# Up projection: product 2 of two neighbouring pairs as seven half-size block products

## The chip, the core and the metric

The kernel runs on one core of a Trainium2 chip. The core has a matrix engine (TensorE, PE in the profile, with its weight loads shown apart as PEld), a vector engine (VectorE, DVE), a scalar engine (ScalarE, ACT), a general one (GpSimd, POOL) and SyncE (SP), which here only issues transfers. Matmul results land in PSUM, eight banks of 512 float32 per partition; all else lives in SBUF or in device memory. The metric is the time of one execution on the device in microseconds, as the median of several runs.

## The reference

Two layers of an encoder over 1040 frames (16 learned ones and 1024 of input) with 1024 channels. In each layer an attention part (gated linear attention and softmax attention) is followed by a gated feed-forward part, and only the latter matters here:

```python
def conv_ffn(x, w_up, conv_w, conv_b, w_down):
    h = x @ w_up                        # 1040 x 1024 times 1024 x 5632
    L = h.shape[1]
    hp = jnp.pad(h, ((0, 0), (CONV_W - 1, 0), (0, 0)))
    hc = conv_b
    for j in range(CONV_W):             # causal, width 3, per channel
        hc = hc + hp[:, j:j + L] * conv_w[j]
    u, g = jnp.split(hc, 2, axis=-1)
    return (jax.nn.silu(g) * u) @ w_down
```

All is float32. The hidden width of 2816 is 22 tiles of 128 channels, once for u and once for g.

## The kernel before

Channels lie on partitions, frames along the free dimension. A float32 product is made of three matmuls in a reduced float32 format (`mm3`, lines 218 to 224): each operand is split into a high part (a cast on ScalarE) and a low part (a subtraction on VectorE), and hi*hi, lo*hi and hi*lo are summed in PSUM.

The up projection of a layer (`ffn_up`, from line 1076) goes over 22 pairs j of a u tile and a g tile. For each pair the product of 256 output channels by 1024 input channels with the 1040 frames is seen as a 2 x 2 block product: output u or g, input channels lower or upper half, frames first or second half (`t0`, `t1`, 520 frames each; 516 in the last layer). It is taken as seven block products p = 1 to 7 in place of eight, by the Strassen-Winograd scheme. One block product has 512 input channels, 128 outputs and 520 frames: four weight blocks of 128 x 128, two pieces of 260 frames, three matmuls each, 24 matmuls in all.

The weight operands of the seven products are A11, A12 (u, lower and upper channels), A22, A21 (g), and the combinations S1, S2 and so on, made on VectorE in `block_operand` (line 1037, the combinations at line 1055) and split in `up_split` (line 1067: the cast at 1072 gives hi, the subtraction at 1073 gives lo). The raw tiles come by SyncE's transfers (line 1045). The moving operands X[1] to X[7] are the same for all pairs, and are made once per layer at its start (`put`, line 1094).

Product 2 is A12 with X[2], the upper channels of the first half of the frames. It goes to u's first half only: C11 = P1 + P2.

The order of PE's work is the list `seq` (lines 1101 to 1107), written out by hand. From the sixth pair on a pair's part of it is

```python
(j, 2), (j, 6), (j, 5), (j, 7), (j + 1, 1), (j, 4), (j, 3)
```

The operand of a product is requested four places ahead in this list (`AHEAD`, `ensure`). Its hi and lo tiles rotate through six pairs of buffers, three in each of two pools by turns, so a split can start when the product six places earlier is done. Raw weight tiles have four buffers (`raw`) for A11 and A12, and seven (`raw2`) for the rest. PE works strictly in the order written; the instructions of the other engines are put in order, ahead of the run, by a planner that simulates them with a cost model, and each engine then works through its own list.

PSUM is four double banks, p0 to p3. Products 1, 6, 7, 4 of a pair accumulate in one double bank ("a", p0 or p1 by turns) and are read after each step; 5 and 3 share p2 ("x"), and 2 has p3 ("y"). The results are taken out by ScalarE copies (line 1264) and VectorE adds (line 1263) into two SBUF tiles, `hu` and `hg`. After product 3 the pair is complete, and `conv` (line 1249) does the width-3 convolution: a ScalarE activation (line 1252) and two VectorE steps (line 1256) for each of u and g, then a SiLU on ScalarE (line 1283), a product on VectorE (line 1287), and a store to device memory (line 1288).

During the last pair the operands that are no longer needed give their SBUF slots back, and `during_last` (`tail` in `ffn_down`) uses them to load and split the first inputs of the down projection (lines 337 and 1381), which follows at once. There are 33 slots of 1040 float32 per partition, and 6 more in this part of the layer; the seven moving operands take 28 of them.

Of the kernel before, what the change touches and what calls it, by code (L numbers as in the profile page):

```python
# [25 lines left out]
NFF = 22  # L26
# [13 lines left out]
M_GK, M_GQ, M_GV, M_GR, M_REM, M_FQ, M_FK, M_FV, M_WO, M_UP = 0, 2, 4, 8, 12, 13, 17, 21, 25, 33  # L40
# [8 lines left out]
GROUPS, LAST = (("n", 0, 3), ("s", 3, 8), ("r", 11, 4), ("r", 15, 4)), (19, 3)  # L49
HALVES, HALVES_LAST, HALVES_OUT = (0, 520, 520), (8, 524, 516), (16, 528, 512)  # L50
AHEAD = 4
NSPLIT = 4
N_DMA_SUM = 5
WARM = 12


# [79 lines left out]
class Kern:  # L136
# [893 lines left out]
    def up_operand(self, lyr, j, p, fw, raws, odd):  # L1030
        if (j, p) in ((2, 1), (2, 2), (3, 2), (4, 2)):
            src = fw.tile([128, 4, 128], F32, tag="raw2", name="raw2")
            self.nc.sync.dma_start(src[:], self.wm[lyr, M_UP + 2 * j][:, 4 * p - 4:4 * p, :])
            return self.up_split(src, fw, odd)
        return self.block_operand(self.wm[lyr, M_UP + 2 * j], self.wm[lyr, M_UP + 2 * j + 1], 4, j, p, fw, raws, odd, j < N_DMA_SUM)

    def block_operand(self, u, g, nk, j, p, fw, raws, odd, by_dma=False):

        nc = self.nc
        if j not in raws:  # L1040
            q = raws[j] = {}
            for name, src, k0, own in (("A11", u, 0, True), ("A21", g, 0, False), ("A22", g, nk, False), ("A12", u, nk, True)):
                q[name] = self.wp.tile([128, 4, 128], F32, tag="raw", name="raw", bufs=4) if own else \
                    fw.tile([128, 4, 128], F32, tag="raw2", name="raw2")
                nc.sync.dma_start(q[name][:, :nk, :], src[:, k0:k0 + nk, :])
            if by_dma:
                q["S1"] = fw.tile([128, 4, 128], F32, tag="raw2", name="raw2")
                nc.sync.dma_start(q["S1"][:], g[:, 0:4, :])
                nc.gpsimd.dma_start(q["S1"][:], g[:, 4:8, :], accum_op=ALU.add)
        q = raws[j]  # L1050
# [25 lines left out]
    def ffn_up(self, lyr, mix, hT, pp, fw, halves, o0, during_last):  # L1076
        nc, s = self.nc, self.slots
        W = halves[2]
        n = W // 2
        sl = [slice(c, c + W) for c in halves[:2]]  # L1080
        gain = lambda k: self.v(lyr, V_FN, k)
        bank2 = lambda name, i: pp.tile([128, 2, 512], F32, tag=f"p{i}", name=name, bufs=1)
# [3 lines left out]
        half_slot = lambda name: s.get(F32, name, (128, 2, 520))  # L1086


        X = {}
# [154 lines left out]
        before = {1: second_half, 2: make_t2, 7: make_t3, 8: make_n4, 11: make_t1, 14: make_b22}  # L1244


        st = {}

        def conv(hb, idx):
            t = s.get(F32, "cv")  # L1250
# [7 lines left out]
            s.put(hb)  # L1258
            return t

        def evacuate(j, p):
            q = st[j]
            add = lambda out, ps: nc.vector.tensor_tensor(out=two(out), in0=used(ps), in1=two(out), op=ALU.add)  # L1263
            copy = lambda out, bank="a": nc.scalar.copy(two(out), used(q[bank]))
            if p in (1, 2):
                bank = "a" if p == 1 else "y"
                if "u" in q:
                    add(q["u"][:, t0], q[bank])
                else:
                    q["u"] = s.get(F32, "hu")  # L1270
                    copy(q["u"][:, t0], bank)
            elif p == 6:
                copy(q["u"][:, t1])
            elif p == 7:
                q["g"] = s.get(F32, "hg")
                copy(q["g"][:, t1])
            elif p == 4:
                copy(q["g"][:, t0])
            elif p == 3:
                add(q["u"][:, t1], q["x"])  # L1280
                u, g = conv(q["u"], j), conv(q["g"], j + NFF)
                uo, go = u[:, o0:T], g[:, o0:T]
                nc.scalar.activation(go, go, AF.Silu)
                if j == NFF - 1:
                    self.preload = self.tc.keep_in_program_order(
                        nc.scalar.preload_act_table_set("natural_log_exp_and_others"))
                nc.vector.tensor_tensor(out=uo, in0=uo, in1=go, op=ALU.mult)  # L1287
                nc.gpsimd.dma_start(self.actd[j][:, o0:T], uo)  # L1288
                s.put(u, g)
                del st[j]  # L1290
# [128 lines left out]
    def down_blocks(self, lyr, g0, ng, X, pp, fw, halves, after):  # L1419
# [345 lines left out]
```

## Time and profile before

| | |
|---|---|
| median of 3 runs | 2515.2 us (2514.78 to 2515.3) |
| the profiled execution | 2518.04 us, span 2516.3 us |
| matmuls | 18442, of which 7392 in the up projection |
| up projection, layer 0 | 568 to 1013 us |
| up projection, layer 1 | 1812 to 2260 us |
| mean granted TensorE clock | 0.996 |

The profile's page gives, for each engine, the busy time and its share of the span. A row of its groups or of the timeline names the line of the program, the engine, the operation, the tiles (written tile first, then an arrow and what is read) and the shape; after a bar stand the busy time, the mean duration and the idle time of the engine just before, with what ended it. A row of the windows gives, for each stretch of time, the busy time and the number of instructions of each engine, the granted clock, the share of the transfer engines and GB/s. Matmul durations overlap, because the engine is pipelined; what counts is the distance from start to start.

### The profile page before, as it was taken

To read this page: it belongs to the slowest core of one execution; us is meant where nothing else is said; L and a number is where in the kernel's file an instruction comes from. 1 tells how busy PE (TensorE), PEld (TensorE's weight loads), DVE (VectorE), ACT (ScalarE), POOL (GpSimd) and SP (SyncE) were. 2 spreads that over 40 slices of the span, in tenths; PEclk is the share of its full clock that TensorE was granted. 3 is DMA by queue.
4 is the path that set the end of the run, shared out by engine and by line. 5 is a ranking of instruction groups with operands and counts; after the bars stand their busy time and mean duration, and the time that the engine had idled before them with its cause. 6 is when DMAs were issued, how large, how long until landed. Compare 5 with 4: busy or idle time off the path is not lost.

```text
span 2516.3 us, 47049 instructions
## 1 busy us (share of the span) xinstructions
PE 2477.9 (98%) x18442; PEld 2383.8 (95%) x18442; DVE 1767.2 (70%) x3523; ACT 1272.9 (51%) x2733; POOL 385.3 (15%) x567
## 2 busy tenths in 40 slices
PE   9999999999999999999999999999999999999998
PEld 8999999999999999999999899999999999997786
DVE  8656777769877777853666666777798777787535
ACT  7346666636544445631443566665464444455312
POOL 2023433210000000100211234331100000001002
PEclk9999999999999999999999999999999999999999
DMA  3232134343322224763312222143433222258722
GB/s 133 67 88 74 44 92 133 118 130 97 119 81 81 77 77 146 193 170 106 107 57 69 74 80 78 58 153 109 142 105 101 76 79 78 80 166 186 194 56 74
DMA packets 118542, 260.94 MB, mean 104 GB/s; under 512 B 14880, under 2 KB 32544, under 8 KB 118320
## 3 DMA queue, kind: packets, MB, share of 16 engines
q1 hardware_dynamic: 93984, 182.79, 23.5%
q0 software_dynamic: 22464, 72.84, 10.4%
q8 instruction: 144, 2.36, 0.4%
q10 hardware_dynamic: 1872, 2.31, 0.3%
q14 instruction: 78, 0.64, 0.1%
HBM read 177.29 MB, written 67.81 MB: 97 GB/s over the span
## 4 chain that ended last, share of the span: by engine, by line
PE 81%; DVE 10%; ACT 4%; DMA 2%; issue 2%; SPq 0%; POOL 0%; DVEq 0%; ACTq 0%; POOLq 0%
PE up L222 11%; PE up L224 11%; PE up L223 11%; PE mm L222 7%; PE mm L224 7%; PE mm L223 7%; PE down L222 5%; PE down L223 5%; PE down L224 5%; PE av L720 3%; PE tr L694 2%; DVE S L661 1%; PE S L658 1%; ACT P L673 1%; PE S L659 1%
## 5 line engine op out<-in xcount | busy, mean ns | idle before, releaser
L222 PE MATMUL up<-x,hi 128*128 128x260 f32 (+1 forms) x2464 | 696.6, 283 | 0.0
L224 PE MATMUL up<-x,hi 128*128 128x260 f32 (+1 forms) x2464 | 695.9, 282 | 0.7 <-DVE x L1097 0.7
L223 PE MATMUL up<-x,lo 128*128 128x260 f32 (+1 forms) x2464 | 696.3, 283 | 0.0
L224 PEld LDWEIGHTS up<-x,hi 128*128 128x128 f32 x2464 | 465.3, 189 | 1.1 <-DVE x L1097 1.1
L222 PEld LDWEIGHTS up<-x,hi 128*128 128x128 f32 x2464 | 464.5, 189 | 0.4 <-DVE hu L1263 0.2
L223 PEld LDWEIGHTS up<-x,lo 128*128 128x128 f32 x2464 | 464.5, 189 | 0.1
L1073 DVE TENSOR_TENSOR lo<-raw,hi 128x512 fp32r<-128x512 f32 x364 | 247.7, 685 | 173.0 <-ACT hi L1072 172.7
L222 PE MATMUL mm<-xh,hi 128*128 128x348 f32 (+4 forms) x1056 | 362.7, 343 | 0.0
L224 PE MATMUL mm<-xl,hi 128*128 128x348 f32 (+4 forms) x1056 | 339.8, 322 | 0.0
L223 PE MATMUL mm<-xh,lo 128*128 128x348 f32 (+4 forms) x1056 | 339.4, 321 | 0.0
L1072 ACT CAST hi<-raw 128x512 fp32r<-128x512 f32 x364 | 223.6, 620 | 128.1 <-PE up L224 84.5
L222 PEld LDWEIGHTS mm<-xh,hi 128*128 128x128 f32 x1056 | 199.5, 189 | 5.2 <-issue 4.6
L223 PEld LDWEIGHTS mm<-xh,lo 128*128 128x128 f32 x1056 | 199.5, 189 | 0.7 <-issue 0.7
L224 PEld LDWEIGHTS mm<-xl,hi 128*128 128x128 f32 x1056 | 198.3, 188 | 0.4 <-issue 0.3
L189 ACT CAST hi<-raw 128x512 fp32r<-128x512 f32 (+2 forms) x168 | 97.4, 581 | 176.0 <-PE down L224 97.0
L223 PE MATMUL down<-ah,lo 128*128 128x260 f32 (+1 forms) x528 | 168.6, 319 | 0.4 <-DVE lo L191 0.3
L224 PE MATMUL down<-al,hi 128*128 128x260 f32 (+1 forms) x528 | 168.5, 319 | 0.0
L222 PE MATMUL down<-ah,hi 128*128 128x260 f32 (+1 forms) x528 | 168.2, 319 | 0.0
L673 ACT ACTIVATE P<-S,m 116x460 f32<-116x460 f32 (+2 forms) x224 | 124.8, 561 | 71.2 <-DVE m L661 67.6
L337 DVE TENSOR_TENSOR PT<-tr,PT 116x464 fp32r<-116x464 f32 (+3 forms) x240 | 122.8, 514 | 46.9 <-ACT PT L336 45.3
L1055 DVE TENSOR_TENSOR raw<-raw,raw 128x512 f32<-128x512 f32 x198 | 129.4, 684 | 17.2 <-DMA raw<-in_wd_dram 16.5
L1288 POOL DMA_DIRECT2D actd<-cv x44 | 23.6, 535 | 756.9 <-DVE cv L1287 735.9
(289 smaller groups left out, 5623.8 us busy)
## 6 DMA issues: line engine op xcount, KB each, us to landing
raw<-in_wm_dram SPq DMA_DIRECT2D x330, 256.0 KB, 2.7
raw<-in_wd_dram SPq DMA_DIRECT2D x64, 256.0 KB, 3.6
actd<-cv POOLq DMA_DIRECT2D x22, 520.0 KB, 3.0
actd<-cv POOLq DMA_DIRECT2D x22, 512.0 KB, 2.9
cb<-cd SPq DMA_DIRECT2D x16, 520.0 KB, 4.1
st<-actd SPq DMA_DIRECT2D x14, 520.0 KB, 4.9
st<-actd SPq DMA_DIRECT2D x14, 512.0 KB, 4.6
kA<-kA SPq DMA_DIRECT2D x24, 260.0 KB, 3.9
```

The source lines that it names most:

```text
L189: nc.scalar.copy(hi[:, :n, :], raw[:, :n, :])
L222: nc.tensor.matmul(ps, wh, xh[:, c0:c0 + n], start=first, stop=False, skip_group_check=more)
L223: nc.tensor.matmul(ps, wl, xh[:, c0:c0 + n], start=False, stop=False, skip_group_check=more)
L224: nc.tensor.matmul(ps, wh, xl[:, c0:c0 + n], start=False, stop=last, skip_group_check=more)
L337: nc.vector.tensor_tensor(out=lo, in0=src, in1=hi.bitcast(F32), op=ALU.subtract)
L658: nc.tensor.matmul(S[:rows, :n], q["qA"][e][:, qs], q["kA"][e][:, c0:k1], start=True, stop=False)
L673: nc.scalar.activation(P[:rows, :n], S[:rows, :n], AF.Exp, scale=-1.0, bias=m[:rows, nch - 1:nch], accum_out=(den if nch == 1 else d3[:row ...
L694: nc.tensor.transpose(tr[:w, 3 - j, :rows], P[:rows, o:o + w], id_)
L720: nc.tensor.matmul(av[:, a:b], w.rearrange("p a b -> p (a b)"), x, start=(t == ts[0] and part == 0 and i == 0), stop=(t == last and i == 1))
L1055: nc.vector.tensor_tensor(out=q[out][:, :nk, :], in0=q[a][:, :nk, :], in1=q[b][:, :nk, :], op=op)
L1072: nc.scalar.copy(hi[:, :nk, :], src[:, :nk, :])
L1073: nc.vector.tensor_tensor(out=lo[:, :nk, :], in0=src[:, :nk, :], in1=hi[:, :nk, :].bitcast(F32), op=ALU.subtract)
```

## The change

From pair 6 on the pairs are taken two by two, j and j + 1. Both products 2 use the same moving operand X[2], so that together they are one product of 256 outputs (u of j and u of j + 1), 512 input channels and 520 frames. This is again a 2 x 2 block product (output pair, 256 channels, 260 frames), and it is taken as seven products of half size, written m(1) to m(7) (20 is added to their number in the list). One has two weight blocks, one piece of 260 frames and three matmuls each: 6 matmuls.

- The seven moving operands: three are parts of X[2]; four (Y) are made once per layer, one instruction group per product during pairs 4 and 5 (`second_level`).
- The weight operands (`sub_operand`): parts of the two A12 tiles, and the combinations in one further `raw2` tile (`s`), two half-size combinations for m(6) and one each for m(7) and m(3); each is split at half size.
- The raw tiles of pair j + 1 are loaded where those of pair j's group begin (`block_raws`), before its own product 1.
- A12 is no longer overwritten by product 3's combination; S2 is.
- The half products have one double bank, p3: m(1), m(6), m(7), m(4) accumulate in its first bank, m(2) alone and then m(5), m(3) in its second. After each (after m(5) only when product 1 of pair j + 1 is out) VectorE adds 260 frames to a quarter of u of j or of j + 1 (`sub_evacuate`).
- The order in a group is m(1), m(2), 6, m(6), 5, m(5), 7, 1 of j + 1, m(7), 4, m(3), 3, m(4), and then 6, 5, 7, 1 of the next, 4, 3 for pair j + 1.
- X[2] and the four Y tiles give their slots back after m(4) of the last group, before product 6 of the last pair; before, X[2] did so after product 2 of the last pair.

```diff
+        src = lambda j: (self.wm[lyr, M_UP + 2 * j], self.wm[lyr, M_UP + 2 * j + 1], 4, j)
+        if p > SUB:
+            self.block_raws(*src(j), fw, raws)
+            self.block_raws(*src(j + 1), fw, raws)
+            return self.sub_operand(raws[j], raws[j + 1], p - SUB, fw, odd)
+        return self.block_operand(*src(j), p, fw, raws, odd, j < N_DMA_SUM)
+
+    def sub_operand(self, q, r, m, fw, odd):
+        A, B = q["A12"], r["A12"]
+        lo, hi = slice(0, 2), slice(2, 4)
+        tt = lambda out, a, b, op: self.nc.vector.tensor_tensor(out=out, in0=a, in1=b, op=op)
+        if m == 6:
+            q["s"] = fw.tile([128, 4, 128], F32, tag="raw2", name="raw2")
+            tt(q["s"][:, lo, :], B[:, lo, :], B[:, hi, :], ALU.add)
+            tt(q["s"][:, hi, :], q["s"][:, lo, :], A[:, lo, :], ALU.subtract)
+        elif m == 7:
+            tt(q["s"][:, lo, :], A[:, lo, :], B[:, lo, :], ALU.subtract)
+        elif m == 3:
+            tt(q["s"][:, hi, :], A[:, hi, :], q["s"][:, hi, :], ALU.subtract)
+        src, at = {1: (A, lo), 2: (A, hi), 3: (q.get("s"), hi), 4: (B, hi), 5: (q.get("s"), lo),
+                   6: (q.get("s"), hi), 7: (q.get("s"), lo)}[m]
+        return self.up_split(src[:, at, :], fw, odd, 2)
...
         elif p == 3:
-            combine("A12", "A12", "S2", ALU.subtract)
-        src = q[{1: "A11", 2: "A12", 3: "A12", 4: "A22", 5: "S1", 6: "S2", 7: "A21"}[p]]
+            combine("S2", "A12", "S2", ALU.subtract)
+        src = q[{1: "A11", 2: "A12", 3: "S2", 4: "A22", 5: "S1", 6: "S2", 7: "A21"}[p]]
...
-        for j in range(3, NFF - 1):
+        for j in range(3, FIRST_SUB):
             seq += ([(j, 2)] if j > 4 else []) + [(j, 6), (j, 5), (j, 7), (j + 1, 1), (j, 4), (j, 3)]
-        seq += [(NFF - 1, p) for p in (6, 5, 7, 2, 4, 3)]
+        for j in range(FIRST_SUB, NFF, 2):
+            m = lambda i: (j, SUB + i)
+            seq += [m(1), m(2), (j, 6), m(6), (j, 5), m(5), (j, 7), (j + 1, 1), m(7), (j, 4), m(3), (j, 3)]
+            seq += [m(4), (j + 1, 6), (j + 1, 5), (j + 1, 7)] + ([(j + 2, 1)] if j + 2 < NFF else [])
+            seq += [(j + 1, 4), (j + 1, 3)]
...
+        def second_level():
+            at0, at1 = slice(0, n), slice(n, W)
+            t = [half_slot("t") for _ in range(2)]
...
+            b11, b12, b21, b22 = (x.t[:, :, at] for x in t for at in (at0, at1))
...
+                def g():
+                    Y[m] = y = s.get(F32R, f"y{m}", (128, 4, 260))
+                    self.split(y.t[:, 0:2, :n], y.t[:, 2:4, :n], out)
+                return [f, g]
+            return [whole(0), whole(1), *make(7, b12, b22, b12, ALU.subtract), *make(6, b11, b12, b11, ALU.add),
+                    *make(5, b22, b22, b11, ALU.subtract), *make(4, b21, b21, b11, ALU.subtract),
+                    lambda: s.put(*t)]
...
+        def sub_evacuate(j, m):
+            bank = sub_bank(m)
+            to, c = {1: (j, 0), 2: (j, 0), 6: (j, 1), 3: (j, 1), 5: (j + 1, 1), 7: (j + 1, 1), 4: (j + 1, 0)}[m]
+            o = st[to]["u"][:, halves[0] + c * n:halves[0] + c * n + n]
+            nc.vector.tensor_tensor(out=o, in0=st[j]["s"][:, bank, :n], in1=o, op=ALU.add)
+        sub_bank = lambda m: 0 if m in (1, 6, 7, 4) else 1
...
+            if (j, p) == (4, 6):
+                building = second_level()
+            if j in (4, 5) and (j, p) != (4, 1) and building:
+                building.pop(0)()
...
+                if m == 1:
+                    q["s"] = bank2("sub", 3)
+                xs, c0 = sub_moving(m)
+                first = m in (1, 2, 5)
+                for k in range(2):
+                    self.mm3(q["s"][:, sub_bank(m), :n], ops[i][k], xs[k], c0, n, first and k == 0, k == 1, not first)
+                ops[i] = None
+                evacuate(j, p)
```

More of the change, by code (lines that the diff above doesn't have):

```diff
@@ L51 @@
 AHEAD = 4
+SUB = 20
 NSPLIT = 4
 N_DMA_SUM = 5
+FIRST_SUB = 6
 WARM = 12
@@ L1034, in up_operand, with block_raws @@
             return self.up_split(src, fw, odd)
-        return self.block_operand(self.wm[lyr, M_UP + 2 * j], self.wm[lyr, M_UP + 2 * j + 1], 4, j, p, fw, raws, odd, j < N_DMA_SUM)
-    def block_operand(self, u, g, nk, j, p, fw, raws, odd, by_dma=False):
+        src = lambda j: (self.wm[lyr, M_UP + 2 * j], self.wm[lyr, M_UP + 2 * j + 1], 4, j)
[19 more added lines that the diff above has]
+        return self.up_split(src[:, at, :], fw, odd, 2)
+    def block_raws(self, u, g, nk, j, fw, raws, by_dma=False):
         nc = self.nc
@@ L1049, in block_operand @@
                 nc.gpsimd.dma_start(q["S1"][:], g[:, 4:8, :], accum_op=ALU.add)
+    def block_operand(self, u, g, nk, j, p, fw, raws, odd, by_dma=False):
+        nc = self.nc
+        self.block_raws(u, g, nk, j, fw, raws, by_dma)
         q = raws[j]
@@ L1244, in ffn_up @@
         before = {1: second_half, 2: make_t2, 7: make_t3, 8: make_n4, 11: make_t1, 14: make_b22}
-        st = {}
+        st, building = {}, []
         def conv(hb, idx):
@@ L1259, in conv, with whole, make, f @@
             return t
+        Y = {}
+        def second_level():
+            at0, at1 = slice(0, n), slice(n, W)
+            t = [half_slot("t") for _ in range(2)]
+            def whole(i):
+                return lambda: nc.vector.tensor_tensor(out=t[i].t[:, :, :W], in0=X[2][0][i].t[:, :, :W].bitcast(F32),
+                                                       in1=X[2][1][i].t[:, :, :W].bitcast(F32), op=ALU.add)
+            b11, b12, b21, b22 = (x.t[:, :, at] for x in t for at in (at0, at1))
+            def make(m, out, a, b, op):
+                def f():
+                    nc.vector.tensor_tensor(out=out, in0=a, in1=b, op=op)
+                def g():
[5 more added lines that the diff above has]
+                    lambda: s.put(*t)]
+        def sub_moving(m):
+            if m in Y:
+                return [(Y[m].t[:, k, :], Y[m].t[:, 2 + k, :]) for k in range(2)], 0
+            i, c0 = {1: (0, 0), 2: (1, 0), 3: (1, n)}[m]
+            return [(X[2][0][i].t[:, k, :], X[2][1][i].t[:, k, :]) for k in range(2)], c0
+        def sub_evacuate(j, m):
[4 more added lines that the diff above has]
+        sub_bank = lambda m: 0 if m in (1, 6, 7, 4) else 1
         def evacuate(j, p):
+            if p > SUB:
+                if p - SUB != 5:
+                    sub_evacuate(j, p - SUB)
+                return
             q = st[j]
@@ L1271, in evacuate @@
                     copy(q["u"][:, t0], bank)
+                if "s" in st.get(j - 1, ()) and p == 1:
+                    sub_evacuate(j - 1, 5)
             elif p == 6:
@@ L1289, in evacuate @@
                 s.put(u, g)
-                del st[j]
+                if "s" not in q:
+                    del st[j]
             q.setdefault("done", set()).add(p)
@@ L1298, in ffn_up @@
                 before[i]()
-            q = st.setdefault(j, {})
+            if (j, p) == (4, 6):
+                building = second_level()
+            if j in (4, 5) and (j, p) != (4, 1) and building:
+                building.pop(0)()
+            if p == SUB + 1:
+                while building:
+                    building.pop(0)()
+            q = st.setdefault(j, {})
+            if p > SUB:
+                m = p - SUB
+                if m == 1:
[6 more added lines that the diff above has]
+                evacuate(j, p)
+                if (j, m) == (NFF - 2, 4):
+                    for x in X.pop(2):
+                        s.put(*x)
+                    s.put(*Y.values())
+                    during_last(2)
+                continue
             bank, first = {2: "y", 5: "x", 3: "x"}.get(p, "a"), p in (1, 2, 5)
```

## The prediction

> **What bounds the kernel now.** I read the page's totals first, then who waited for whom on PE inside the two up-projection stretches, then busy time by stage, and last the order of VectorE's and ScalarE's work around one pair's end.
>
> ```profile
> PE 2477.9 (98%) x18442; PEld 2383.8 (95%) x18442; DVE 1767.2 (70%) x3523; ACT 1272.9 (51%) x2733; POOL 385.3 (15%) x567
> ...
> PE up L224 <- DVE x L1097: 0.2, 1, 0.2
> ...
> PE up L224 <- DVE x L1097: 0.5, 1, 0.5
> ```
>
> The first line is the totals; the other two are everything PE waited for between 568 and 1013 us (layer 0) and between 1811 and 2260 us (layer 1): 0.7 us in some 890. The up stage is PE's, end to end. What a matmul costs there:
>
> ```profile
> core 0: us, PE busy (x) PEld busy (x) DVE busy (x) ACT busy (x) POOL busy (x), PEclk, DMA share, GB/s
> 568.00:657.00 89.00, 88.81 (x731) 88.15 (x730) 88.23 (x130) 54.03 (x85) 5.74 (x8) 1.00 0.39 115
> 657.00:695.00 38.00, 38.00 (x320) 38.00 (x319) 28.88 (x37) 18.90 (x29) 1.06 (x2) 1.00 0.25 85
> 695.00:735.00 40.00, 40.00 (x337) 40.00 (x336) 29.46 (x39) 19.39 (x28) 1.06 (x2) 1.00 0.23 80
> ...
> 700.00:980.00 280.00, 280.00 (x2346) 280.00 (x2346) 206.22 (x265) 136.57 (x197) 7.44 (x14) 1.00 0.25 86
> 1902.00:1940.00 38.00, 38.00 (x319) 38.00 (x318) 28.25 (x36) 19.02 (x28) 1.06 (x2) 1.00 0.24 80
> 1940.00:2240.00 300.00, 300.00 (x2498) 300.00 (x2497) 219.60 (x284) 143.38 (x210) 7.97 (x15) 1.00 0.27 90
> ```
>
> In the steady stretch of layer 0, 2346 matmuls take 280 us: 119.4 ns each, product boundaries included; in layer 1 2498 take 300 us: 120.1 ns. The granted clock is 1.00. (The durations of 282 ns in the page's groups overlap and are no price.) A whole product, 24 matmuls, is 2.87 us. VectorE is 74% busy and ScalarE 49%, so both have room, but not much on VectorE.
>
> **The change, part by part.** (a) *Matmuls.* Product 2 of two pairs is 2 x 24 matmuls. Its replacement is 7 products x 2 K-blocks x 3 matmuls = 42, of the same width (260 or 258). Six fewer in each of 8 groups in each layer: 48 x 119.4 ns + 48 x 120.1 ns = 5.73 + 5.76 = 11.5 us. This is the whole gain, and all of it lies on the path.
>
> Is the pitch a cost of the matmul or of the boundary between products? Seven boundaries take the place of two in each group, so this matters.
>
> ```profile
> 700.18 0.28 PE L222 MATMUL up<-x,hi 128*128 128x260 f32 x1
> 700.30 0.28 PE L223 MATMUL up<-x,lo 128*128 128x260 f32 x1
> 700.42 0.28 PE L224 MATMUL up<-x,hi 128*128 128x260 f32 x1
> 700.54 0.28 PE L222 MATMUL up<-x,hi 128*128 128x260 f32 x1
> ```
>
> Inside one product the starts are 0.12 us apart, as the mean over all, so a boundary costs nothing that shows. [...]
>
> (b) *Operands and evacuations.* The prices:
>
> ```profile
> L1073 DVE TENSOR_TENSOR lo<-raw,hi 128x512 fp32r<-128x512 f32 x364 | 247.7, 685 | 173.0 <-ACT hi L1072 172.7
> L1072 ACT CAST hi<-raw 128x512 fp32r<-128x512 f32 x364 | 223.6, 620 | 128.1 <-PE up L224 84.5
> ...
> L1263 DVE TENSOR_TENSOR hu<-up,hu 128x520 f32<-128x520 f32 x44 | 30.4, 692 | 0.0
> L1287 DVE TENSOR_TENSOR cv<-cv 128x1040 f32<-128x1040 f32 x22 | 27.1, 1233 | 0.0
> L1611 DVE TENSOR_TENSOR h<-mm,h 128x256 f32<-128x256 f32 x24 | 9.5, 412 | 2.6 <-PE mm L224 2.6
> L723 ACT COPY avs<-av 128x232 f32<-128x232 f32 x64 | 22.7, 354 | 4.8 <-PE av L720 3.9
> ```
>
> VectorE starts the next instruction about 0.08 us before the end of one (0.69 us long, 0.61 apart, in the timeline below), so 0.61 for a full operation and 0.33 for a half one (412 - 80 ns). Per group it loses two lo subtractions and two adds of 520, 4 x 0.61 = 2.4 us. It gains seven half lo subtractions, four half combinations (two for product 6, one each for 7 and 3) and seven half adds out of PSUM: 18 x 0.33 = 5.9 us. Net +3.5 us: 29.5 + 3.5 = 33 us busy in 39.4, or 84%. ScalarE: seven half casts of about 0.38 us (between 354 ns at 232 and 620 ns at 512) for two of 0.62: +1.4 us. Both are beside PE as long as PE never has to wait; without that cover the cost is what the rivals price.
>
> (c) *The moving operands, once per layer.* During pairs 4 and 5: two sums of 1040, four combinations and four splits of 520, 2 x 1.15 + 8 x 0.61 = 7.2 us on VectorE (four casts on ScalarE). This falls into the stretches 657 to 695 us and 1902 to 1940 us, where it makes VectorE 28.9 + 7.2 = 36.1 of 38 us (28.3 + 7.2 = 35.5 in layer 1): 95%. The stretch before (568 to 657) leaves VectorE full, 88.2 of 89. So it enters the first group with some backlog. Between nothing and the whole remainder of the backlog (2 to 3 us a layer, rival 3) I take 0.5 us a layer, 1.0 in all, near nothing because nothing in that stretch waits today.
>
> (d) *Order, PSUM, buffers.* Four things now have to arrive in time.
>
> ```profile
> 734.55 1.30 DVE L1256 SCALAR_TENSOR_TENSOR cv<-hg,vec,cv 128x1039 f32<-128x1039 f32 x1 [0.46 <-ACT cv L1252]
> 735.77 0.69 DVE L1263 TENSOR_TENSOR hu<-up,hu 128x520 f32<-128x520 f32 x1
> 736.38 1.29 DVE L1256 SCALAR_TENSOR_TENSOR cv<-hg,vec,cv 128x1038 f32<-128x1038 f32 x1
> 737.58 0.69 DVE L1073 TENSOR_TENSOR lo<-raw,hi 128x512 fp32r<-128x512 f32 x1
> 738.19 1.30 DVE L1256 SCALAR_TENSOR_TENSOR cv<-hu,vec,cv 128x1039 f32<-128x1039 f32 x1
> 739.40 0.69 DVE L1263 TENSOR_TENSOR hu<-up,hu 128x520 f32<-128x520 f32 x1
> 740.01 1.29 DVE L1256 SCALAR_TENSOR_TENSOR cv<-hu,vec,cv 128x1038 f32<-128x1038 f32 x1
> 741.22 0.68 DVE L1073 TENSOR_TENSOR lo<-raw,hi 128x512 fp32r<-128x512 f32 x1
> 741.82 1.23 DVE L1287 TENSOR_TENSOR cv<-cv 128x1040 f32<-128x1040 f32 x1
> ...
> 735.13 0.62 ACT L1072 CAST hi<-raw 128x512 fp32r<-128x512 f32 x1 [0.61 <-PE up L224]
> 736.50 1.26 ACT L1252 ACTIVATE cv<-hu,vec 128x1040 f32<-128x1040 f32 x1 [0.75 <-DVE hu L1263]
> ```
>
> Product (j,3) of a pair ends at about 735.1 (the cast at 735.13 was released by it). Then VectorE works through that pair's convolution: two steps per half, the product at L1287, with operand subtractions and the add of the next product 2 (739.40) between them. In the new order a group begins here: half products 1 and 2 (0.72 us each), product (j,6) (2.87 us), then half product 6, which accumulates in the same bank as half product 1 and so waits for that one's add. It is wanted at 735.1 + 0.72 + 0.72 + 2.87 = 739.4. The add is ready at 735.9. VectorE is in the second hg step until 737.58, and the next step needs ScalarE's activation of hu, which ends at 736.50 + 1.26 = 737.76; the hole at 737.58 is filled by an unrelated subtraction today. The add is issued earlier in the program than that subtraction, so I expect it in this hole, done by 738.0, 1.4 us ahead. Cost taken: nothing. The other reuses have 3.6 us or more (half product 3 after 5's add, wanted a half and a whole product after (j+1,1)).
>
> Operands: six buffer pairs rotate, so a cast can start when the product six places earlier is over, five products ahead: 14.3 us today. In a group the shortest such stretch is two whole and three half products, 7.9 us. After a cast and a subtraction (1.3 us) 6.6 us are left, against a VectorE that is behind by 1 to 3 us in the burst above. Cost taken: nothing.
>
> Weights: the raw tiles of pair j+1 are loaded with pair j, three half-length steps ahead of their first use and still some 10 us before PE wants them; SP queues nothing else here, and a tile lands in 2.7 us:
>
> ```profile
> raw<-in_wm_dram SPq DMA_DIRECT2D x330, 256.0 KB, 2.7
> ...
> 1043.38 0.68 DVE L1073 TENSOR_TENSOR lo<-raw,hi 128x512 fp32r<-128x512 f32 x1
> ...
> L222 PEld LDWEIGHTS down<-x,hi x336: 186/188/330, 1047.6 to 2376.7; 128*128 128x128 f32 x168
> ```
>
> End of the stage: VectorE is behind there, and the down projection's first block product (1047.6) has its operand ready at 1044.1, 3.5 us early. Product (21,2) is gone from the last pair (-2.87 us of PE), while three half products now follow (21,1), where the preparation of the down projection begins (+2.15 us); with some 0.8 us more on VectorE the slack falls by about 1.5 us and stays positive. Cost: nothing. Half product 3's operand in its own buffer instead of A12 is the same number of instructions: nothing.
>
> **Sum.** -11.5 + 1.0 = -10.5 us. The profiled execution (2518.04 us, of which 2516.3 span and 1.7 around it) should go to 2507.5 with a span of 2505.8. The median of the runs, 2515.2, lies 2.8 us under the profiled one; taken from it, 2504.7.
>
> **Rivals.** 1. *The burst blocks half product 6.* VectorE runs in the order written, so the add of half product 1 waits for all that stands ahead. [...] If it stands where product 2's add stands today (739.40, done 739.8), PE loses 0.4 to 0.5 us in each of 16 groups, 6.4 to 8 us: 2511 to 2513, no change. If it stands behind the second hu step (done 741.6), 2.2 us, 35 us: 2540. Behind L1287 (743.05, done 743.4), 4.0 us, 64 us: 2569. The point from which it decides is 10.5 / 16 = 0.66 us a group. For it: VectorE has no idle time between 734.55 and 743. Against it: the hole at 737.58.
>
> 2. *Operands late.* If product (j,7)'s subtraction stands behind the whole burst and the extra half operations it ends at about 744.6, and PE wants it at 743.7: 0.9 us x 16 = 14 us, 2519. VectorE's 84% speaks for it, the 6.6 us left speak against. [...]
>
> 3. *The entry is dearer.* 2 to 3 us a layer: 2508 to 2510.
>
> 4. *A boundary costs after all.* The three steps quoted in (a) sum to 0.36 us, read to 0.01: 117 ns at the least within a product. The rest of the mean, 2.4 ns x 24 = 0.06 us a boundary, times 5 more boundaries x 16 groups would be 4.6 us: 2509. [...]
>
> **How the numbers follow.** Forecast (2503 to 2508): 0.57. Rival 3: 0.10. Rival 4: 0.03. Rival 1 at its mild place: 0.11, of which 0.09 no change; in its dear places: 0.10, slower. Rival 2: 0.09, 0.04 of it no change and 0.05, where it takes more than a microsecond a group, slower. With 0.2% as 5.0 us (2510.2 and 2520.2, about what a measurement of this kernel can tell from no change): faster 0.57 + 0.10 + 0.03 + 0.02 = 0.72, same 0.13, slower 0.15. The low end is no wait anywhere, 2503.7, less 0.7 for scatter: 2503. The high end takes in rivals 3, 4 and the mild 1: 2513, which leaves out 0.19.
>
> **What would show it.** PE with 18346 matmuls; about 39.4 us for two pairs in place of 40.1; no wait of PE at the group's third half product; VectorE at about 84% in the steady stretch. A repeated wait "up <- DVE hu" of more than 0.7 us, or PE waiting for lo, would make it wrong.

## The result, and the profile after

The changed kernel takes 2599.4 us (median; 2598.67 to 2600.39), 1.0335 times the kernel before [1.032 to 1.035]: 84 us more, where 10.5 us less was forecast. The profiled execution took 2600.39 us, its span is 2598.5 us.

The page of the changed kernel, its totals:

```profile
PE 2493.0 (96%) x18346; PEld 2390.2 (92%) x18346; DVE 1849.4 (71%) x3767; ACT 1306.4 (50%) x2821; POOL 386.0 (15%) x567
```

The 96 matmuls are gone as counted, and VectorE and ScalarE have the added instructions. What PE waited for in the whole span, changed kernel (total us, times, longest):

```profile
PE sub L224 <- DVE hu L1328: 59.6, 32, 2.6
PE down L225 <- DVE lo L193: 4.5, 2, 2.4
...
PE up L225 <- DVE lo L1102: 1.5, 2, 0.8
PE up L224 <- ACT hg L1338: 1.4, 2, 0.7
```

The first line is new: 32 waits, two in each of 16 groups, all before a half product (`sub`), all released by the add of a half product (line 1328, `sub_evacuate`). The busy time by stretch, changed kernel:

```profile
core 0: us, PE busy (x) PEld busy (x) DVE busy (x) ACT busy (x) POOL busy (x), PEclk, DMA share, GB/s
657.00:695.00 38.00, 38.00 (x320) 38.00 (x319) 33.12 (x47) 20.36 (x33) 1.06 (x2) 1.00 0.22 71
700.00:980.00 280.00, 258.49 (x2074) 256.00 (x2074) 211.30 (x327) 129.41 (x205) 6.91 (x13) 0.97 0.22 75
743.90:747.20 3.30, 3.30 (x17) 3.30 (x17) 3.30 (x5) 0.62 (x1) 0.00 (x0) 0.50 0.00 0
1950.00:2250.00 300.00, 279.00 (x2251) 276.50 (x2250) 231.27 (x354) 142.38 (x224) 7.45 (x14) 0.98 0.22 72
```

PE was never idle in 700 to 980 us before; now it is idle for 21.5 us there, and the granted clock is 0.97 as a mean. The third row shows why the clock is low: in a stretch of 3.3 us behind one of the waits it is 0.50. One group's beginning on PE, changed kernel (start, duration, [idle before and its releaser]):

```profile
739.79 0.28 PE L224 MATMUL sub<-x,hi 128*128 128x260 f32 x1
...
740.39 0.28 PE L226 MATMUL sub<-x,hi 128*128 128x260 f32 x1
743.12 0.39 PE L224 MATMUL sub<-x,hi 128*128 128x260 f32 x1 [2.45 <-DVE hu L1328]
...
744.04 0.42 PE L224 MATMUL up<-x,hi 128*128 128x260 f32 x1
744.26 0.42 PE L225 MATMUL up<-x,lo 128*128 128x260 f32 x1
...
747.28 0.28 PE L224 MATMUL up<-x,hi 128*128 128x260 f32 x1
747.40 0.28 PE L225 MATMUL up<-x,lo 128*128 128x260 f32 x1
...
758.29 0.28 PE L226 MATMUL up<-x,hi 128*128 128x260 f32 x1
759.71 0.39 PE L224 MATMUL sub<-y,hi 128*128 128x260 f32 x1 [1.14 <-DVE hu L1328]
...
784.96 0.28 PE L224 MATMUL sub<-x,hi 128*128 128x260 f32 x1
```

Half product 1 is the six matmuls from 739.79. Half product 2, which writes the *other* bank of p3 and needs nothing of half product 1, begins 2.73 us after the last of them. Half product 7 (759.71, first bank) comes 1.42 us late, held by the add of half product 5 (second bank). Between the two, matmuls start 0.22 us apart for a while, not 0.12. The next group begins at 784.96, 45.17 us after this one. VectorE at the same place:

```profile
740.84 0.69 DVE L1337 TENSOR_TENSOR hu<-up,hu 128x520 f32<-128x520 f32 x1
741.45 1.28 DVE L1289 SCALAR_TENSOR_TENSOR cv<-hg,vec,cv 128x1038 f32<-128x1038 f32 x1
742.65 0.42 DVE L1328 TENSOR_TENSOR hu<-sub,hu 128x260 f32<-128x260 f32 x1
742.99 1.29 DVE L1289 SCALAR_TENSOR_TENSOR cv<-hu,vec,cv 128x1039 f32<-128x1039 f32 x1
...
759.23 0.43 DVE L1328 TENSOR_TENSOR hu<-sub,hu 128x260 f32<-128x260 f32 x1 [1.84 <-ACT hu L1338]
```

The add (742.65) does stand in the hole behind the second hg step, where the prediction put it: half product 1 is over at 740.67, and VectorE still does that step (741.45), which stands ahead in its list, before the add. PE stands still until the add is over (743.07, half product 2 at 743.12). The add at 759.23 follows ScalarE's copy of u of pair j + 1, and that copy follows product 1 of j + 1.

From start to start, first to last matmul of each up projection, worked out from all its matmuls (us):

```
                        layer 0: before  after   layer 1: before  after
whole stage                      444.8   484.9            448.2   486.0
96 matmuls fewer                         -5.7                     -5.8
gaps before half products          0     33.8               0     33.1
other gaps                         0.5    2.5               1.0    4.0
starts 0.22 us apart, excess       1.4   11.0               1.3    9.5
```

The gap rows count every step of more than 0.3 us. Eight steps of 0.38 us among them (2.1 us over the pitch in all) lie inside stretches at half clock (0.50) and belong rather to the last row. Of the last row, the 1.4 and 1.3 us of the kernel before are not half clock, which its up stages don't have: a dozen matmuls of the norm behind the first product start 0.2 us apart, in both kernels.

The stages are 40.1 and 37.8 us longer, 77.9 of the 82.2 us that the span grew.

### The profile page after: what moved, and what is told of

The parts are those of the page before. It is cut to its first block, busy times and chain, and to the rows that moved or that the text cites. A ratio compares the mean times of both kernels' runs of the same rounds, so it can differ in the third digit from the quotient of the medians.

```text
span 2598.5 us, 47403 instructions
## 1 busy us (share of the span) xinstructions
PE 2493.0 (96%) x18346; PEld 2390.2 (92%) x18346; DVE 1849.4 (71%) x3767; ACT 1306.4 (50%) x2821; POOL 386.0 (15%) x567
## 4 chain that ended last, share of the span: by engine, by line
PE 47%; issue 32%; DVE 13%; ACT 5%; DMA 2%; POOL 1%; SPq 0%; DVEq 0%; POOLq 0%; ACTq 0%
PE mm L224 7%; PE mm L226 6%; PE mm L225 6%; PE down L224 5%; PE down L225 5%; PE down L226 5%; PE av L722 3%; PE tr L696 2%; DVE S L663 1%; PE S L660 1%; PE wo L224 1%; PE wo L226 1%; PE wo L225 1%; PE S L661 1%; DVE cv L1289 1%
## 5 line engine op out<-in xcount | busy, mean ns | idle before, releaser
L224 PE MATMUL up<-x,hi 128*128 128x260 f32 (+1 forms) x2208 | 630.2, 285 | 2.3 <-ACT hg L1338 1.4
L225 PE MATMUL up<-x,lo 128*128 128x260 f32 (+1 forms) x2208 | 629.1, 285 | 1.5 <-DVE lo L1102 1.5
L226 PE MATMUL up<-x,hi 128*128 128x260 f32 (+1 forms) x2208 | 628.0, 284 | 0.5 <-DVE x L1126 0.5
L224 PEld LDWEIGHTS up<-x,hi 128*128 128x128 f32 x2208 | 422.5, 191 | 3.4 <-ACT hg L1338 1.8
L225 PEld LDWEIGHTS up<-x,lo 128*128 128x128 f32 x2208 | 422.0, 191 | 2.0 <-DVE lo L1102 1.9
L226 PEld LDWEIGHTS up<-x,hi 128*128 128x128 f32 x2208 | 422.2, 191 | 1.0 <-DVE x L1126 1.0
L1101 ACT CAST hi<-raw 128x512 fp32r<-128x512 f32 (+1 forms) x444 | 250.2, 567 | 182.4 <-PE up L226 87.9
L1102 DVE TENSOR_TENSOR lo<-raw,hi 128x512 fp32r<-128x512 f32 (+1 forms) x444 | 269.6, 620 | 95.3 <-ACT hi L1101 94.0
L1084 DVE TENSOR_TENSOR raw<-raw,raw 128x512 f32<-128x512 f32 x198 | 134.2, 689 | 24.0 <-DMA raw<-in_wd_dram 21.5
```

Source lines behind the costliest of these rows:

```text
L224: nc.tensor.matmul(ps, wh, xh[:, c0:c0 + n], start=first, stop=False, skip_group_check=more)
L225: nc.tensor.matmul(ps, wl, xh[:, c0:c0 + n], start=False, stop=False, skip_group_check=more)
L226: nc.tensor.matmul(ps, wh, xl[:, c0:c0 + n], start=False, stop=last, skip_group_check=more)
L1101: nc.scalar.copy(hi[:, :nk, :], src[:, :nk, :])
L1102: nc.vector.tensor_tensor(out=lo[:, :nk, :], in0=src[:, :nk, :], in1=hi[:, :nk, :].bitcast(F32), op=ALU.subtract)
```

## The experiments

**Theory A:** both banks of p3 are one PSUM tile, and the program's waits are laid for the tile; PE waits for adds from the bank that it doesn't touch. **Theory B:** VectorE is too full or its order too late, and the half products would wait for their adds, operands or order in any case. The first four runs tell these apart.

**Two tiles.** p3 becomes two tiles of one bank, in all stages; additions and copies out of a whole p3 become two instructions.

```diff
+def psum2(pp, i, name):
+    if i == 3:
+        return Two([pp.tile([128, 512], F32, tag=f"p3{c}", name=name, bufs=1) for c in "ab"])
+    return pp.tile([128, 2, 512], F32, tag=f"p{i}", name=name, bufs=1)
...
-                    self.mm3(q["s"][:, sub_bank(m), :n], ops[i][k], xs[k], c0, n, first and k == 0, k == 1, not first)
+                    self.mm3(bank_of(q["s"], sub_bank(m), n), ops[i][k], xs[k], c0, n, first and k == 0, k == 1, not first)
```

> The double bank p3 as two tiles of one bank each, wherever it is used; the order and all else as in the change (adds and copies out of p3 become two of 260, half as many per bank). Theory A: in the change the wait of half product 2 for half product 1's add, and of half product 7 for half product 5's, are no need of the data. They come because both banks are one tile, so that a read of one bank holds back a write to the other. Then both waits go here, PE waits for the half products' adds less than 5 us in all, the clock stays at 1.00 through the up projection, and the time is 2504 to 2509. Theory B: VectorE is simply late with its adds, or the two banks disturb each other in the chip. Then the gap of 2.6 us ahead of half product 2 or an equal one ahead of half product 6 stays, and the time is above 2580.

Measured 2514.7 us, 0.9989 [0.998, 0.9998]. The longest waits of PE here:

```profile
PE down L247 <- DVE dg L1567: 3.9, 2, 2.0
PE down L248 <- DVE lo L216: 3.7, 2, 2.3
...
PE up L247 <- ACT hg L124: 1.4, 2, 0.7
```

No line "sub" is left, although both banks are written and read by turns as before: A holds, the waits were the tile's. The up stages take 440.9 and 444.7 us, 3.9 and 3.5 less than before. The time missed the expected one all the same (2504 to 2509), which the later runs follow.

**Spread order.** One tile, but always a whole product between two half products.

```diff
-            seq += [m(1), m(2), (j, 6), m(6), (j, 5), m(5), (j, 7), (j + 1, 1), m(7), (j, 4), m(3), (j, 3)]
-            seq += [m(4), (j + 1, 6), (j + 1, 5), (j + 1, 7)] + ([(j + 2, 1)] if j + 2 < NFF else [])
+            seq += [m(1), (j, 6), m(2), (j, 5), m(6), (j, 7), m(5), (j + 1, 1), (j, 4), m(3), (j, 3), m(7)]
+            seq += [(j + 1, 6), (j + 1, 5), m(4), (j + 1, 7)] + ([(j + 2, 1)] if j + 2 < NFF else [])
```

> The change with one tile as it is, but no half product stands behind another in the list: 1h, 6, 2h, 5, 6h, 7, 5h, 1 of the next pair, 4, 3h, 3, 7h, 6, 5, 4h, 7, 1, 4, 3 (h for half). Theory A: each add now has a whole product (2.87 us) before the next write to the tile. The add of half product 1 ends 2.6 us after it in the change's trace, so the waits go or shrink to a few tenths; time 2505 to 2515. Theory B: the waits follow the half products to their new places; time above 2560.

Measured 2530.59 us, 1.0049 [1.0035, 1.0063]. Its waits before half products:

```profile
PE sub L224 <- ACT hi L1101: 4.1, 8, 0.5
...
PE sub L224 <- DVE hu L1328: 3.2, 8, 0.4
```

59.6 us of waiting for adds became 3.2, without any tile split: time between the half products helps as well, as A says. But the new order brings waits for operands (the first line), and the time missed the expectation by 15 us. The up stages take 447.6 and 450.0 us, 2.8 and 1.8 more than before; the other 8 us lie outside them, 6.1 of these between the two stages, and were not followed.

**Half spread.** As above, with half product 7 left right behind product 1 of j + 1 (and 4, 3 in their old places).

```diff
+            seq += [m(1), (j, 6), m(2), (j, 5), m(6), (j, 7), m(5), (j + 1, 1), m(7), (j, 4), m(3), (j, 3)]
```

> As the change, but half products 1, 2, 6 and 5 are moved so that a whole product stands between them (1h, 6, 2h, 5, 6h, 7, 5h, 1 of the next pair, 7h, 4, 3h, 3, 4h, 6, 5, 7, 1, 4, 3). Half product 7 still comes right after product 1 of the next pair, where half product 5's add is made. Theory A: the 2.6 us wait at half product 2 goes in all 16 groups (42 us, and most of the half-speed clock with it), the 1.3 us wait at half product 7 stays (21 us): 2525 to 2540. Theory B: little changes, above 2570.

One execution: 2552.91 us, above what was expected.

```profile
PE sub L224 <- DVE hu L1328: 28.4, 32, 2.6
```

The gap before half product 2 is gone. The one before half product 7 is left: 1.42 us in 14 groups, 2.9 us in the last group of each layer. Half product 6 now waits 0.4 to 0.5 us in every group, some 7 us in all, which the expectation did not have. With only the order changed, one of the two long waits goes and one stays.

**Half as many groups** (from pair 14 on).

```diff
-FIRST_SUB = 6
+FIRST_SUB = 14
```

> The change from pair 14 on only: 4 groups a layer in place of 8; the moving operands are made in pairs 4 and 5 as before. If the loss is one of each group (theory A, two waits and a slowed clock per group), it halves: 84 x 4/8 = 42 us over the kernel before, 2553 to 2561. If it were the entry (making the moving operands) or the end of the stage, it would stay near 84: above 2580.

One execution: 2563.45 us, 46 us above the kernel before (2517.72 on that chip), for 84 with twice the groups, and 2.5 us above the expected range. Most of the loss goes with the groups. By these two points some 8 us would not (2 x 46 less 84), so something done once per layer may carry a small part.

After these, A stood, and the open question was why the mended kernel gains about 3 us and not 10. Three suspects: the last pairs, the S2 buffer, and the split of p3 in the other stages.

**The last pair.** Two tiles, and half product 4 of the last group moved behind product 7, so that a product stands again between products 7 and 4 of the last pair.

```diff
+            last = j + 2 == NFF
+            seq += ([] if last else [m(4)]) + [(j + 1, 6), (j + 1, 5), (j + 1, 7), m(4) if last else (j + 2, 1)]
```

> The two-tile kernel with one more edit: in the last group half product 4 moves from ahead of the last pair's product 6 to between its products 7 and 4, where product 2 stood before the change; with it moves the point where X[2] and the Y tiles give their slots back and the down projection's preparation goes on. In the two-tile trace PE waits 0.7 us in each layer for ScalarE's copy of product 7 (hg) ahead of product 4, since nothing stands between them now, and 2.3 and 1.4 us in the first down products for the low part of a weight (lo), which VectorE makes behind preparation that starts earlier than before the change. Theory: the end of the stage is what is left of the loss. Then both waits go to a few tenths, 4 to 6 us are won, and the time is 2508 to 2511. Rival: VectorE has too much to do at the end wherever it starts; then only the hg wait goes: 2512 to 2514.

Measured 2519.79 us, 1.0012 [1.0003, 1.002]: above the theory's range and the rival's.

```profile
PE down L248 <- DVE lo L216: 4.6, 5, 1.7
...
PE up L247 <- ACT hg L124: 0.5, 2, 0.4
```

The wait for hg fell from 1.4 to 0.5 us, and as much came back as waits for lo in the down projection, five instead of two (4.6 us for 3.7). That the median is also some 5 us above that of two tiles, on another chip, these waits don't explain; the profiled execution (2516.62 us) is one of the fastest.

**Own S2 alone.** The kernel before, with only product 3's combination in S2.

```diff
-            combine("A12", "A12", "S2", ALU.subtract)
+            combine("S2", "A12", "S2", ALU.subtract)
```

> The kernel before with one part of the change alone: product 3's combination is written to S2 and not over A12. If this is what makes PE wait in the first products of the stage (about 1 us more in each layer than before: a gap of 1.2 us at the eighth product of layer 0), the same gap shows here and the time is 1 to 3 us above the kernel before. If not, the trace of the early products is that of before.

One execution: 2515.53 us, within the spread of the kernel before (2513.81 to 2518.86 on that chip): the time does not show a cost, the trace does. What it waited for in the up projection of layer 0, and where:

```profile
PE up L223 <- DVE lo L1073: 0.8, 1, 0.8
...
591.66 0.39 PE L223 MATMUL up<-x,lo 128*128 128x260 f32 x1 [0.78 <-DVE lo L1073]
```

This is product 6 of the second pair (j = 1), the eighth product of the stage. The wait, of 0.2 to 0.8 us, is in every kernel with this edit and in none without it, and the gaps of its up stages sum to 1.6 and 1.7 us, against 0.5 and 1.0. Why the subtraction comes later there is not settled.

**Old S2.** As "the last pair", with the combination over A12 again.

```diff
-            combine("S2", "A12", "S2", ALU.subtract)
+            combine("A12", "A12", "S2", ALU.subtract)
```

> The kernel with the last-pair edit, with product 3's combination over A12 again, as before the change (A12 has been read by all half products of its group that need it by then). If the S2 edit costs, 1 to 3 us less than the last-pair kernel; if not, within a microsecond of it.

Measured 2518.14 us, 1.0005 [0.9996, 1.0014]; the early wait is gone, and the time is 1.6 us below that of "the last pair", which is no more than the scatter of the two (each spreads over some 6 us).

**Banks only.** The kernel before with p3 as two tiles.

> A control: the kernel before with p3 as two tiles and nothing else, no half products. The adds and copies out of p3 become two of 260 in place of one of 520, in every product 2 of the later pairs too (0.33 x 2 against 0.61 us). No PE wait should come of it: within 2 us of the kernel before.

One execution: 2517.11 us, against 2516.55 for the kernel before. The split costs little. Its trace is 1.7 us behind by the middle of layer 0's down projection, but only 0.4 of it is a new wait. The rest is a stretch at half clock from 1129.7 us, behind a wait of 1.9 us for dg that the kernel before has too (its matmul at 1128.67), there at a granted clock of 1.00 all through (1127.27 to 1134.10 us).

**Last two pairs plain.** Two tiles, seven groups in a layer, the last two pairs as before.

```diff
-        for j in range(FIRST_SUB, NFF, 2):
+        for j in range(FIRST_SUB, NFF - 2, 2):
...
+        j = NFF - 2
+        seq += [(j, 2), (j, 6), (j, 5), (j, 7), (j + 1, 1), (j, 4), (j, 3)]
+        seq += [(NFF - 1, p) for p in (6, 5, 7, 2, 4, 3)]
```

> The two-tile kernel with 7 groups a layer: the last two pairs are done as before the change, with whole products 2, and X[2] is given back where it was before; only the Y tiles are given back earlier. Six matmuls a layer return, so 84 fewer than before the change, 84 x 0.1198 = 10.1 us. Theory: what the two-tile kernel gives back is at the end of the stage, where PE now reaches the first down products before VectorE has prepared them (2.3 and 1.4 us for a lo, 0.7 and 0.7 for hg, and the half-speed clock after them). With the old end these waits are those of before, and the time is 2508 to 2511. Rival: VectorE's work at that point sets the time at which the down projection can start, however early PE comes; then PE waits there whatever the last pairs look like, and the time stays at 2513 to 2517.

Measured 2514.09 us, 0.9983 [0.9973, 0.9992]; single executions between 2510.1 and 2519.25. That is the rival's range. The profiled one is the fastest of them (2510.1). Its waits for lo at the seam, where the down projection follows the up projection:

```profile
PE down L248 <- DVE lo L216: 2.3, 2, 1.2
```

Less waiting at the seam than with eight groups (3.7) in one trace of each, but no clear gain in the time. An eighth group saves 0.7 us a layer by its matmuls; that it costs about as much at the end is a guess that fits.

**Last two plain, p3 whole outside the groups, old S2.**

```diff
+    def tile(self, name):
+        self.use("double")
+        return self.pool.tile([128, 2, 512], F32, tag="p3", name=name, bufs=1)
+
+    def pair(self, name):
+        self.use("pair")
+        return [self.pool.tile([128, 512], F32, tag=f"p3{c}", name=name, bufs=1) for c in "ab"]
```

> As the kernel with the last two pairs plain, but p3 is two one-bank tiles only while half products run; before and after it is one double bank again, so no add or copy elsewhere is cut in two, and product 3's combination is written over A12 as before the change. If cutting the adds costs (the control showed 1.7 us in the down projection) and the S2 edit costs a little, this is 1 to 4 us less than that kernel: 2505 to 2509, or by the rival there 2511 to 2515.

Measured 2515.22 us, 0.9989 [0.9981, 0.9998]: at the end of the rival's range, and no better than its parts.

**The change, mended.** The changed kernel as it is, order and S2 included; only p3 is two tiles while the groups run, and whole elsewhere (the two functions above).

```diff
-                    q["s"] = bank2("sub", 3)
+                    q["s"] = self.p3.pair("sub")
...
-                    self.mm3(q["s"][:, sub_bank(m), :n], ops[i][k], xs[k], c0, n, first and k == 0, k == 1, not first)
+                    self.mm3(q["s"][sub_bank(m)][:, :n], ops[i][k], xs[k], c0, n, first and k == 0, k == 1, not first)
```

> The smallest repair of the change: all as in the change, 8 groups a layer and its order, only p3 is two one-bank tiles while half products run, and a double bank before and after. Beside the two-tile kernel it leaves out the adds that are cut in two. Theory as for that kernel: no wait at half products 2 and 7, and the time is 0 to 3 us below its 2514.7: 2511 to 2515.

Measured 2513.88 us (2512.16 to 2515.0), 0.9982 [0.9973, 0.999]; the kernel before had 2518.06 on that chip. That is as expected: 4.2 us (0.2%) below the kernel before, a small gain, though its interval leaves out 1, and 86 us below the change, which ran on another chip. Its windows, and its PE and VectorE at the group shown above:

```profile
core 0: us, PE busy (x) PEld busy (x) DVE busy (x) ACT busy (x) POOL busy (x), PEclk, DMA share, GB/s
700.00:980.00 280.00, 280.00 (x2343) 280.00 (x2342) 237.36 (x369) 145.55 (x234) 7.46 (x14) 1.00 0.26 84
1960.00:2240.00 280.00, 280.00 (x2337) 280.00 (x2337) 235.91 (x370) 147.28 (x236) 7.46 (x14) 1.00 0.28 90
...
735.62 0.28 PE L249 MATMUL sub<-x,hi 128*128 128x260 f32 x1
...
739.94 0.28 PE L249 MATMUL sub<-y,hi 128*128 128x260 f32 x1
...
775.13 0.28 PE L249 MATMUL sub<-x,hi 128*128 128x260 f32 x1
...
738.48 0.42 DVE L1353 TENSOR_TENSOR hu<-sub,hu 128x260 f32<-128x260 f32 x1
```

PE is never idle, the group takes 39.51 us, and half product 6 (739.94) finds the add of half product 1 done 1.0 us earlier (738.90). What is left of waits:

```profile
PE down L250 <- DVE lo L218: 3.5, 2, 2.0
...
PE up L250 <- DVE lo L1127: 1.5, 2, 0.8
PE up L249 <- ACT hg L1363: 1.4, 2, 0.7
...
1025.35 0.39 PE L250 MATMUL down<-ah,lo 128*128 128x260 f32 x1 [2.04 <-DVE lo L218]
1026.20 0.42 PE L250 MATMUL down<-ah,lo 128*128 128x260 f32 x1
1026.41 0.42 PE L251 MATMUL down<-al,hi 128*128 128x260 f32 x1
```

Its up stages take 441.4 and 443.7 us, 7.9 us less than before in sum. Then 3.6 us are lost at the start of layer 0's down projection: a gap of 2.32 us from start to start (2.2 over the pitch) before 1025.35, and behind it 17 matmuls 0.22 us apart, 0.1 us too much each, together about 1.6 us. These make up the balance of the span, 2512.0 against 2516.3; smaller losses and gains elsewhere about cancel.

## Why the prediction was wrong

**(a) Matmuls: right.** 18346, and with the waits away 39.51 us for two pairs (39.4 forecast, 40.1 before). A boundary between products costs next to nothing: the group is 0.1 us above the forecast, where rival 4 would have added 0.3.

**(b) Operands and evacuations: right.** VectorE 237.4 of 280 us without the waits, 84.8% (84 forecast), and PE doesn't wait for it in the steady stretch. Rival 2 didn't come.

**(c) The moving operands: right.** VectorE rose from 28.9 to 33.1 of 38 us in that stretch (36.1 forecast); two sums and a combination, 2.9 us by the prediction's prices, had been done just before it, in the stretch that was called full. PE has no wait in that stretch; rival 3 didn't come.

**(d) Order, PSUM, buffers: the step that failed.** It says that half product 6 "accumulates in the same bank as half product 1 and so waits for that one's add", and goes through the reuses of each bank. That is what the data need, and that add comes in the hole that was forecast. But the two banks are one tile, and by the program's waits a write to it also waits for the last read of the other bank. So the first to wait is half product 2, which has no product between it and half product 1, and then half product 7, for the add of half product 5 in the other bank. The group shown loses 2.61 + 1.30 us (2.73 and 1.42 less one pitch of 0.12) and some 1.75 us to the clock: 45.17 - 39.51 = 5.66 us, where rival 1 put the point that decides at 0.66. Rival 1 waits for the right add, but at half product 6, and because it comes late, which it didn't; its dear places, 2540 and 2569, leave out both the second wait and the clock. That they point to "slower" is right in direction only. The sign that the prediction named, a repeated wait of PE for VectorE's hu, came, under the name "sub" in place of "up".

**The clock was not in the sum.** 17.8 us of the loss (11.0 + 9.5 less 1.4 + 1.3) are matmuls at a granted clock of 0.50, and 2.1 us more that the table counts as gaps.

**End of the stage, "nothing": wrong by some 5 us.** In the mended kernel: waits for hg of 1.4 us, and 3.6 us (1.6 of them the clock) and 1.4 us (layer 1's share of the 3.5) at the first down products; the last is offset by less waiting, and a slow stretch less, elsewhere in layer 1. The slack of 3.5 us was to fall by 1.5; VectorE, at 55.2 of 60 us there before (980 to 1040 us) and 57.3 now, gave back more. That VectorE is the cause is argued from this and from "the last pair", where half a product moved to please ScalarE came back as lo waits; no run took VectorE work away there, so the cause stays open.

```profile
980.00:1040.00 60.00, 59.98 (x502) 59.77 (x501) 55.23 (x61) 39.58 (x56) 5.93 (x8) 1.00 0.71 187
```

```profile
980.00:1040.00 60.00, 57.28 (x464) 56.87 (x463) 57.30 (x69) 41.53 (x58) 5.94 (x8) 0.97 0.79 209
```

The first row is the kernel before, the second the mended one.

**S2, "nothing": wrong by 0.7 to 1.1 us a layer** in the gaps of the up stage ("own S2 alone"); the early wait goes again with "old S2". In the times it is lost in the scatter.

So with the waits away, about 8 of the 11.5 us appear in the up stage, and 4 in the time. The forecast of 2504.7 would have been too low even then.

## What to carry to other kernels

When two banks of PSUM are to be written and read by turns, ask what the program's waits are laid on: if both are one tile, a matmul into the one waits for the read of the other, and short products make that wait visible: here 59.6 us in 32 waits, with half products of 0.72 us. Give each bank a tile of its own (none of these waits was left), or put a long product between (3.2 us were left with 2.87 us between). And price a repeated gap of a few microseconds on PE with what follows it on the clock, not with its length alone: here that was 1.8 us more as a mean (17.8 + 2.1 us over 11 slow stretches), where a slow stretch followed a gap of 2.64 to 2.93 us.

## What the hardware showed

In the up stages of the changed kernel, 11 of the 18 gaps of 2.64 to 2.93 us on PE, mostly those of every second group, are followed by about 3.4 us in which matmuls start 0.22 us apart at a granted clock of 0.50 (the row of 743.90 to 747.20), and none of the 14 gaps of 1.42 us is. "Half spread" has, in its up stages, shorter gaps and two of 2.9 us; only behind these two are slow stretches, and the mean granted clock of its whole execution is 0.996, against 0.990 in the changed kernel.

The trace's rows of the granted clock show which gaps these are. Each of the 11 slow stretches lasts 3.41 us, and all begin on one grid with steps of 3.413 us: those that begin at 699.45, 743.83 and 788.20 us are 13 steps apart each time. Here is the changed kernel by such steps, first at the gap of 2.73 us shown above, then at the equally long one before 833.37 us, which has no slow stretch behind it:

```profile
740.41:743.83 3.42, 0.97 (x8) 0.76 (x7) 3.42 (x5) 2.88 (x3) 0.00 (x0) 1.00 0.00 0
743.83:747.24 3.41, 3.41 (x18) 3.41 (x17) 3.41 (x6) 0.69 (x2) 0.00 (x0) 0.50 0.00 0
...
829.16:832.57 3.41, 1.75 (x15) 1.54 (x14) 3.38 (x5) 2.28 (x4) 0.00 (x0) 1.00 0.00 0
832.57:835.98 3.41, 2.61 (x21) 2.62 (x22) 3.41 (x5) 2.18 (x3) 0.00 (x0) 1.00 0.00 0
```

The first gap lies within one step: PE is idle for 2.45 us of it, and the next step is at 0.50. The second is cut by the grid into 1.66 and 0.80 us of idling, and the clock stays at 1.00, in the step behind it (835.98 to 839.40 us) too. So it is with all 18 in this trace: before the 11 slow stretches stands a step with 1.94 to 2.45 us of idling, and in the other seven cases no step has more than 1.72. What tells the two cases apart here is thus how much of the gap falls into one step, and for these gaps that is a matter of where they happen to lie. In the traces of the kernel before and of the changed one, between 12 and 2490 us, every slow stretch follows a step with at least 1.71 us of idling; a step with 1.71 us has one behind it (35.01 to 38.42 us, kernel before), one with 1.72 us has none (1006.65 to 1010.06 us, changed kernel). This is read from the traces; no run moved a gap against the grid.

In the mended kernel a gap of 2.32 us (1023.03 to 1025.35 us) is followed by 17 matmuls 0.22 us apart, and the granted clock of 980 to 1040 us is 0.97 as a mean, where the kernel before has 1.00.

Not settled: whether VectorE's work alone sets the start of the down projection, and where the time goes that "spread order" loses outside the up stages.
